# Empty bytes between the tiles in SBUF: weights and activations at multiples of 128 bytes

## The chip, the cores and the metric

The kernel runs on one core of one Trainium2 chip. The metric is the device time of one execution in microseconds, and the kernel before is given with the median of three runs. All arithmetic on the data happens on the chip; the host only puts the inputs into the order in which the chip reads them.

## The reference

What is computed is a trunk of two layers over 256 tokens of 2048 channels. Each layer has a modulation made from a vector `c`, a sub-layer with two attentions side by side, and a gated MLP with a short convolution over the tokens. Cut to what matters here:

```python
for l in range(2):
    mod = silu(c) @ ada_w[l] + ada_b[l]                    # 2048 x 12288
    sh_a, sc_a, gt_a, sh_m, sc_m, gt_m = split(mod, 6)
    h = rmsnorm(x, norm_mix[l]) * (1 + sc_a) + sh_a
    qa, ka, va, qb, kb, vb, ga, gb = split_cols(h @ w_in[l])   # 2048 x 8704
    ya = window_attention(...) @ w_proj_a[l]               # 8 heads, 2 key heads, rotary, sink
    yb = neighbourhood_attention(...) @ w_proj_b[l]        # 8 heads, learned bias
    x = x + gt_a * ((sigmoid(ga) * ya + sigmoid(gb) * yb) @ w_out[l])
    h = rmsnorm(x, norm_ffn[l]) * (1 + sc_m) + sh_m
    g, v = split(depthwise_conv(h @ w_up[l], conv_w[l], conv_b[l]))   # 2048 x 11264
    x = x + gt_m * ((silu(g) * v) @ w_down[l])             # 5632 x 2048
```

All inputs and the output are float32.

## The kernel before

**Products in two halves.** Every large product is made of 128 x 128 blocks of weights. A float32 number is split into a float32r half "hi" (a copy that the scalar engine rounds) and a rest "lo" (what the vector engine has left after subtracting hi). A block's product is then hi·hi + lo·hi + hi·lo, three products of 256 tokens. `unit` (line 216) loads 16 blocks, 1 MB, in one DMA to a tile `w` of pool `raw` (four buffers, 8192 bytes a partition each) and splits them into two tiles `hl` of pool `hl`, each 128 x 2 x 1024: line 225 is the copy on ScalarE, line 226 the subtraction on VectorE.

**Three forms of the product.**
- `feature_block` without `joint` (lines 239 to 243): the weights are the stationary operand, the activations the moving one. One matmul has 512 columns (hi of the weights with hi and lo of the activations, lines 240 and 242), the other 256 (lo of the weights with hi of the activations, lines 239 and 243). The two are called a pair below.
- `feature_block` with `joint` (lines 235 to 237): three matmuls of 256 columns into one place in PSUM. Most of layer 0's attention sub-layer is done so.
- `tokens` (lines 317 to 319): here 128 tokens of the activations are the stationary operand and 512 output features of the weights the moving one. q, k and v are made so.

The small products of the attention (`sc` line 465, `tp` line 490, `po` line 496, `qtp` line 453) are plain float32 without a split.

**Where operands lie.** Pools are laid out in SBUF one after the other in the order in which they are opened, and each tile takes its bytes rounded up to a multiple of 32. Ahead of the large tiles the pool `const` holds `ident`, `mean`, `mhalf` and the three tiles `cpad` of 1032 bytes, which end at byte 4896 of a partition. From there on nearly everything has a size that is a multiple of 128, so that all following tiles share one remainder; only pool `sm`, with its many tiles of 32 bytes, shifts the pool `s` behind it. The start addresses of the tiles, in bytes within a partition, with their remainders by 128:

| tile | pool | begins at | mod 128 |
|---|---|---|---|
| `ident` | const | 1152 | 0 |
| `cpad` 0, 1, 2 | const | 1728, 2784, 3840 | 64, 96, 0 |
| `cact`, `x` | const | 4896, 13088 | 32 |
| `w`, `aw` (four buffers) | raw | 37920 and on | 32 |
| `hl` (four buffers) | hl | 70688 and on | 32 |
| `h`, `merged` | h | 103456 | 32 |
| `u`, heads 6 and 7 of `oA`, `z`, `r` | ev | 136224 and on | 32 |
| `qsq`, `qn`, `p`, `pT`, `bias` | at | 147488 and on | 32 |
| `oA` (heads 0 to 5), `oB`, `act`, `ya`, q, k and v (`pack`) | s | 163296 and on | 96 |

Blocks within `hl` lie 512 bytes apart, hi and lo 4096; the channels' chunks of `h`, `merged`, `act`, `oA` and `oB` lie 2048 bytes apart, their hi and lo 1024. So each operand of a matmul has the remainder of its tile.

**Order of the work.** Layers, and stages within a layer, follow one another: q, k, v and gates A (in layer 0 in four parts of the rows, since its modulation is still on its way), projection A, gates B, projection B with the merge, `w_out`, and three groups of up and down of the MLP. The modulation (`ada`, line 152) is a product with a vector on VectorE (line 162, a 1 MB load `aw` each), 192 in all, spread over the units of weights by `ADA_PLAN_0` and `ADA_PLAN_1`. The steps of the attention are spread over units too (`Paced`). All loads are issued from SyncE's queue, in the order in which the program asks for them, and `w` and `aw` share the four buffers of `raw`.

Of the kernel before, what the change touches and what calls it, by code (L numbers as in the profile page):

```python
# [9 lines left out]
F32 = mybir.dt.float32  # L10
# [5 lines left out]
P = 128  # L16
# [15 lines left out]
# w_in's columns in groups of 512, in the order of use: k|v of A, q of A, then k, v, q of B by halves  # L32
QKV_GROUPS = [1024, 0, 512, 2560, 3584, 1536, 3072, 4096, 2048]
GATE_A, GATE_B = 4608, 6656
# the FFN's chunks of 128 channels, in groups that are kept on chip between up and down
FF_SIZES = [15, 16, 13]
FF_GROUPS = [list(range(sum(FF_SIZES[:i]), sum(FF_SIZES[: i + 1]))) for i in range(3)]
# the row blocks of q, k, v and mixer A's gates in the parts that are summed at a time: the first layer's modulation
# is still on its way
K_PARTS_0 = [2, 4, 5, 5]  # L40
K_PARTS = [[range(sum(K_PARTS_0[:i]), sum(K_PARTS_0[: i + 1])) for i in range(len(K_PARTS_0))], [range(KC)]]
# the output chunks of w_out and w_down that are worked on at a time: the first ones leave time for the last inputs
FIRST_TURN = 3
OUT_TURNS = [range(0, FIRST_TURN)] + [[mo] for mo in range(FIRST_TURN, KC)]
# chunks of the modulation that are done at a unit of weights, by layers, as corners of a line over the units
ADA_PLAN_0 = [(38, 32), (58, 48), (76, 66), (84, 70), (96, 80), (128, 96), (145, 108), (175, 118), (192, 124), (230, 143)]
ADA_PLAN_1 = [(0, 143), (76, 169), (84, 165), (95, 176), (129, 192)]
# layers whose mixer's products are summed in one place, for want of time on the vector engine
JOINT = [True, False]
# the same, with h, for the first layer's first chunks  # L50
# [3 lines left out]
# products without use that keep the tensor engine's clock up while it waits: before sums, their spread, and h  # L54
# [6 lines left out]
# heads of attention per unit of weights  # L61
ATT = [1.288, 0.4]
ATT_B = [0.21, 0.21]
# the order of the modulation's columns, in chunks of 128
# [4 lines left out]
def block_stream(l):  # L69
    """A layer's weights as (matrix, row block, column block of 128), in the order of use."""  # L70
    seq = []
    for part in K_PARTS[l]:
        for g in QKV_GROUPS:
            for kc in part:
                seq += [("w_in", kc, g // P + j) for j in range(4)]
        for mo in range(KC):
            seq += [("w_in", kc, GATE_A // P + mo) for kc in part]
    for mo in range(KC):
        seq += [("w_proj_a", kc, mo) for kc in range(HA)]
    for mo in range(KC):  # L80
        seq += [("w_in", kc, GATE_B // P + mo) for kc in range(KC)]
    for mo in range(KC):
        seq += [("w_proj_b", kc, mo) for kc in range(HB)]
    for mos in OUT_TURNS:
        seq += [("w_out", kc, mo) for kc in range(KC) for mo in mos]
    for gi, chunks in enumerate(FF_GROUPS):
        cols = [c + h * FC for c in chunks for h in range(2)]
        if gi == 0:
            for kc in range(KC):
                seq += [("w_up", kc, m) for m in cols[:4]]  # L90
            cols = cols[4:]
        for m in cols:
            seq += [("w_up", kc, m) for kc in range(KC)]
        for mos in OUT_TURNS:
            seq += [("w_down", kc, mo) for kc in chunks for mo in mos]
    return seq
# [8 lines left out]
def encoder(ctx: ExitStack, tc: tile.TileContext, a: dict, out: bass.AP):  # L105
    nc = tc.nc
    pool = lambda name, bufs, **kw: ctx.enter_context(tc.tile_pool(name=name, bufs=bufs, **kw))
    const = pool("const", 1)
# [17 lines left out]
    for i in range(3):  # L126
        t = const.tile([P, S + 2], F32, name=f"cpad{i}")
        nc.vector.memset(t[:], 0.0)
        cpad.append(t)

# [13 lines left out]
    x = const.tile([P, KC, S], F32, name="x")  # L144
    sp = pool("s", 1)
# [6 lines left out]
    def ada(l):  # L152
        """mod[l] = silu(c) @ ada_w[l] + ada_b[l], 128 columns a step, with the columns on partitions"""
        mod = lay.tile([P, 96], F32, name=f"mod{l}", tag="mod")
        ab = load(a["ab"][l], [P, 96], f"ab{l}", lay, tag="ab")
        nrm = load(a["nrm"][l], [P, 2, KC], f"nrm{l}", lay, tag="nrm")
        amod = lay.tile([P, 2, KC], F32, name=f"amod{l}", tag="amod")
        mods[l], amods[l] = mod, amod
        for n, i in enumerate(ADA_ORDER):
            raw = rawp.tile([P, D], F32, name=f"aw{l}_{n}", tag="raw")  # L160
            nc.sync.dma_start(raw[:], a["aw"][l, n])
            nc.vector.tensor_tensor_reduce(  # L162
                out=raw[:], in0=raw[:], in1=cact[:], scale=1.0, scalar=ab[:, i : i + 1],
                op0=ALU.mult, op1=ALU.add, accum_out=mod[:, i : i + 1],
            )
            part, kc = divmod(i, KC)
            if part in (1, 4):
                w = part // 3
                nc.vector.scalar_tensor_tensor(
                    out=amod[:, w, kc : kc + 1], in0=mod[:, i : i + 1], scalar=1.0, in1=nrm[:, w, kc : kc + 1],  # L170
                    op0=ALU.add, op1=ALU.mult,
                )
            done[l] = n + 1
            yield

    class Paced:
        """Steps of generators spread over the units of weights."""
# [4 lines left out]
        def defer(self, fn):  # L182
            """Puts a step off to the next unit"""
            self.later.append(fn)
# [31 lines left out]
    def unit(l, u):  # L216
        """A unit of weights: loaded, and split in two float32r halves (as they are wanted)."""
        raw = rawp.tile([P, UB * P], F32, name=f"w{l}_{u}", tag="raw")
        nc.sync.dma_start(raw[:], a["ws"][l, u])
        halves = []  # L220
        for j in range(2):
            n = UB * P // 2
            hl = hlp.tile([P, 2, n], F32R, name=f"hl{l}_{u}_{j}", tag="hl")
            r = raw[:, j * n : (j + 1) * n]
            nc.scalar.copy(hl[:, 0], r)  # L225
            nc.vector.tensor_tensor(out=hl[:, 1], in0=r, in1=hl[:, 0].bitcast(F32), op=ALU.subtract)  # L226
            halves.append(hl)
        return halves

    def feature_block(ps, hl, j, act, first, last, joint):  # L230
        """One 128 x 128 block: ps[:, :256] += hi.hi + lo.hi, and ps[:, 256:] (or the same place, if joint) += hi.lo."""
# [13 lines left out]
    class Stream:  # L245
        """The layer's units, in order; act(kc) is [P, 2, S] (hi, lo)."""
# [8 lines left out]
        def feed(self, i):  # L255
            """Has the steps of the coming inputs made, a few ahead"""
            while self.steps and self.fed <= i + FEED:
                if next(self.steps, bg) is bg:
                    self.steps = None
                self.fed += 1  # L260

        def prefetch(self, n):
            """Units that are split before what follows"""
            for _ in range(n):
                self.ahead.append(unit(self.l, self.u + len(self.ahead)))

        def hold(self, ins, n):
            """The next n units' splits follow an instruction"""
            self.after = (ins, self.u + len(self.ahead) + n)
# [21 lines left out]
        def features(self, acts, evacs, late=None, joint=False):  # L291
            """Some blocks of 128 output features over the given K blocks, side by side; late() near their end."""
# [13 lines left out]
        def tokens(self, h, kcs):  # L306
            """512 output features of all tokens over the given K blocks, tokens on partitions."""
# [25 lines left out]
    def warm(n):  # L333
        """Products without use: the tensor engine's clock falls when it waits for long"""
        if n:
            ps = ax.tile([P, 512], F32, name="warm", tag="ax")
            for _ in range(n):
                tc.keep_in_program_order(nc.tensor.matmul(ps[:, :P], ident[:], ident[:], start=True, stop=True))

    class Squares:  # L340
        """The tokens' mean squares of x, chunk by chunk; the last one's are apart"""
# [25 lines left out]
    def rsqrt(dst, src, n, k):  # L367
        """dst = (src / n + eps) ** -0.5, in place of a table's square root"""
# [3 lines left out]
    def normed(l, w, sums, st, first=False):  # L372
        """rmsnorm(x) * norm * (1 + scale) + shift, split in halves: the tile, and the steps that fill it"""
# [39 lines left out]
    def qk_rows(pss, heads, rot, gain, dst, then):  # L413
        """q or k of some heads: rmsnorm, rotary, to dst [P (channels), heads, S], a step per unit"""
# [46 lines left out]
    def attend(qT, kT, v, mask, scale, sink, o):  # L461
        """One head, in three steps: o [P (channels), 2, S] from qT, kT [P (channels), S] and v(key block) [P (tokens), channels]"""
# [53 lines left out]
    def plan(l, u):  # L516
        """Goes on with the modulation as planned for a layer's unit"""
# [6 lines left out]
    def need(l, n):  # L524
        """Goes on with the modulation up to the n-th chunk of a layer"""
        while done[l] < n:
            next(adas)

    def ada_and_h(steps):
        """The first layer's modulation, and h chunk by chunk behind it"""  # L530
# [12 lines left out]
    # the tokens' mean squares of the first x  # L543
# [16 lines left out]
    def small(l):  # L560
        """A layer's small inputs"""
# [20 lines left out]
    for l in range(L):  # L582
# [15 lines left out]
        # q, k, v: k|v and q of A, then k, v, q of B by halves  # L598
# [38 lines left out]
        def attention():  # L637
            """The heads' steps, those of a few heads at a time, the oldest head first"""
# [22 lines left out]
        for pi, part in enumerate(parts):  # L661
# [38 lines left out]
            # mixer A's gates  # L700
# [14 lines left out]
        # merge of the branches  # L715
        joint = JOINT[l]

        def whole(ps):
            """The sum of a bank's halves"""
# [42 lines left out]
        def residual(ps, mo, part, joint):  # L762
            """x += gate * ps"""
# [26 lines left out]
        # channel mixer  # L790
# [154 lines left out]
```

## Time and profile before

| | |
|---|---|
| median of 3 runs | 2792.53 us (2791.72 to 2793.07) |
| span of the profiled execution | 2791.1 us |
| instructions | 39852 |
| VectorE busy | 2216.8 us (79%) |
| ScalarE busy | 1449.7 us (52%) |
| DMA | 699.72 MB, 251 GB/s over the span |

The span runs from the first to the last instruction of one profiled execution; the median is of other executions without a profile. A profile of this kernel is best read by stages, since the loads of the modulation and the three forms of the product make each stage different. Rows of matmuls give a start and a modelled duration; successive matmuls overlap, so that the time which one takes is read from the distance between starts.

### The profile page before, as it was taken

The page shows a single profiled execution, that of the slowest core. Times are in us where ns is not written, and L with a number is a line of the kernel's source. Part 1 is how long each engine was busy: PE and PEld are TensorE (multiplying, and loading weights), DVE is VectorE, ACT ScalarE, POOL GpSimd, SP SyncE. Part 2 cuts the span into 40 slices and gives each one's busy share as a digit, 9 for nine tenths or more (in the row PEclk, how much of TensorE's full clock was granted, in tenths as well). Part 3 has the DMA queues.
Part 4 walks back from the last instruction along what each step waited for, and adds up shares of the span by engine and source line. Part 5 has one row for each costly group of instructions (what it writes and reads, how often), then busy time and mean ns, then how long its engine had stood idle before and what let it go on. Part 6 is the DMA issues. An engine that isn't in the chain of part 4 may idle for free.

```text
span 2791.1 us, 39852 instructions
## 1 busy us (share of the span) xinstructions
PE 2734.8 (98%) x15930; PEld 2398.0 (86%) x15930; DVE 2216.8 (79%) x3163; ACT 1449.7 (52%) x2137; POOL 39.3 (1%) x24
## 2 busy tenths in 40 slices
PE   7899999999999999999999999999999999999999
PEld 5788899998888888888878888888878888888888
DVE  6998987897998888789876666768889757766775
ACT  5334784444654555355444567545455535543553
POOL 0000100000000000000000000000000000000000
PEclk9999999999999999999999999999999999999999
DMA  8886588896778766677756666575768655555553
GB/s 313 336 331 254 221 304 326 328 341 231 287 277 320 267 251 252 253 282 282 279 198 238 226 224 238 215 269 195 294 231 290 230 194 181 187 190 181 189 189 136
DMA packets 101852, 699.72 MB, mean 251 GB/s; under 512 B 12705, under 2 KB 15009, under 8 KB 17697
## 3 DMA queue, kind: packets, MB, share of 16 engines
q1 hardware_dynamic: 101666, 697.17, 67.8%
q8 instruction: 125, 2.05, 0.3%
q14 instruction: 61, 0.50, 0.0%
HBM read 695.03 MB, written 2.10 MB: 250 GB/s over the span
## 4 chain that ended last, share of the span: by engine, by line
PE 79%; issue 14%; DVE 4%; POOL 1%; DMA 1%; ACT 1%; POOLq 0%; SPq 0%; DVEq 0%
PE ps L242 33%; PE ps L243 17%; PE ps_t L318 4%; PE ps_t L319 4%; PE ps_t L317 4%; PE ps L236 4%; PE ps L235 4%; PE ps L237 4%; PE ps L240 2%; DVE aw L162 1%; PE ps L239 1%; DVE hl L226 1%; POOL qrs L370 1%; PE sc L465 1%; PE po L496 0%
## 5 line engine op out<-in xcount | busy, mean ns | idle before, releaser
L226 DVE TENSOR_TENSOR hl<-w,hl 128x1024 fp32r<-128x1024 f32 x928 | 1131.8, 1223 | 319.7 <-ACT hl L225 314.5
L225 ACT CAST hl<-w 128x1024 fp32r<-128x1024 f32 x928 | 973.3, 1051 | 778.2 <-PE ps L243 249.0
L242 PE MATMUL ps<-h,hl 128*128 128x512 f32 x3120 | 1113.1, 400 | 0.9 <-DVE h L406 0.9
L243 PE MATMUL ps<-h,hl 128*128 128x256 f32 x3120 | 877.8, 281 | 0.0
L242 PEld LDWEIGHTS ps<-h,hl 128*128 128x128 f32 x3120 | 588.0, 188 | 136.7 <-DVE h L406 1.5
L243 PEld LDWEIGHTS ps<-h,hl 128*128 128x128 f32 x3120 | 590.7, 189 | 9.3
L162 DVE CUSTOM_DVE_ANT_0 aw<-aw,cact,ab 128x2048 f32<-128x2048 f32 x192 | 450.7, 2347 | 19.5 <-DMA aw<-in_aw 19.3
L326 ACT COPY r<-ps 128x256 f32<-128x256 f32 x240 | 89.1, 372 | 302.1 <-PE ps L240 301.9
L317 PE MATMUL ps_t<-hl,h 128*128 128x512 f32 x576 | 228.3, 401 | 7.5 <-ACT hl L225 7.0
L318 PE MATMUL ps_t<-hl,h 128*128 128x512 f32 x576 | 228.8, 397 | 4.7 <-DVE hl L226 4.7
L319 PE MATMUL ps_t<-hl,h 128*128 128x512 f32 x576 | 227.4, 395 | 0.9 <-DVE h L406 0.9
L242 PE MATMUL ps<-act_o,hl 128*128 128x512 f32 x496 | 177.5, 397 | 0.0
L806 DVE SCALAR_TENSOR_TENSOR u<-cpad,cw,u 128x256 f32<-128x256 f32 x352 | 169.1, 482 | 4.8 <-ACT u L804 0.4
L766 DVE SCALAR_TENSOR_TENSOR x<-ps,mod,x 128x256 f32<-128x256 f32 x237 | 111.6, 481 | 47.8 <-PE ps L240 37.4
L237 PE MATMUL ps<-h,hl 128*128 128x256 f32 x512 | 146.1, 285 | 0.0
L235 PE MATMUL ps<-h,hl 128*128 128x256 f32 x512 | 145.4, 284 | 0.0
L236 PE MATMUL ps<-h,hl 128*128 128x256 f32 x512 | 145.2, 284 | 0.0
L243 PE MATMUL ps<-act_o,hl 128*128 128x256 f32 x496 | 139.7, 282 | 0.0
L242 PE MATMUL ps<-act_b,hl 128*128 128x512 f32 x384 | 136.8, 397 | 0.0
L317 PEld LDWEIGHTS ps_t<-hl,h 128*128 128x128 f32 x576 | 109.7, 191 | 31.1 <-ACT hl L225 7.6
L318 PEld LDWEIGHTS ps_t<-hl,h 128*128 128x128 f32 x576 | 110.1, 191 | 30.6 <-DVE hl L226 8.1
L319 PEld LDWEIGHTS ps_t<-hl,h 128*128 128x128 f32 x576 | 109.9, 191 | 24.2 <-DVE h L406 1.4
(214 smaller groups left out, 3998.0 us busy)
## 6 DMA issues: line engine op xcount, KB each, us to landing
w<-in_ws SPq DMA_DIRECT2D x464, 1024.0 KB, 4.9
aw<-in_aw SPq DMA_DIRECT2D x192, 1024.0 KB, 4.9
bias<-in_bias SPq DMA_DIRECT2D x16, 256.0 KB, 4.5
x<-in_xT SPq DMA_DIRECT2D x4, 512.0 KB, 5.6
out<-x SPq DMA_DIRECT2D x16, 128.0 KB, 1.8
cw<-in_cw SPq DMA_DIRECT2D x2, 176.0 KB, 4.5
maskA<-in_maskA SPq DMA_DIRECT2D x1, 256.0 KB, 7.5
ab<-in_ab SPq DMA_DIRECT2D x2, 48.0 KB, 6.1
```

What stands on the lines that cost most here:

```text
L162: nc.vector.tensor_tensor_reduce(out=raw[:], in0=raw[:], in1=cact[:], scale=1.0, scalar=ab[:, i : i + 1], op0=ALU.mult, op1=ALU.add, accum ...
L225: nc.scalar.copy(hl[:, 0], r)
L226: nc.vector.tensor_tensor(out=hl[:, 1], in0=r, in1=hl[:, 0].bitcast(F32), op=ALU.subtract)
L235: nc.tensor.matmul(out[:, 0], hi, act[:, 0], start=first, stop=False)
L236: nc.tensor.matmul(out[:, 0], hi, act[:, 1], start=False, stop=False)
L237: nc.tensor.matmul(out[:, 0], lo, act[:, 0], start=False, stop=last)
L242: nc.tensor.matmul(out, hi, act, start=first, stop=False)
L243: nc.tensor.matmul(out[:, 0], lo, act[:, 0], start=False, stop=False)
L317: nc.tensor.matmul(ps[:], xh, hi, start=kc == kcs[0], stop=False)
L318: nc.tensor.matmul(ps[:], xh, lo, start=False, stop=False)
L319: nc.tensor.matmul(ps[:], xl, hi, start=False, stop=kc == kcs[-1])
L806: nc.vector.scalar_tensor_tensor(out=u, in0=pad[:, o : o + S], scalar=w[:, j : j + 1], in1=u, op0=ALU.mult, op1=ALU.add)
```

## The change

Two tiles that hold nothing of use are put in: one of 96 bytes at the end of the small constants, behind `cpad`, and one of 64 bytes in a pool of its own, opened after all pools but `s`. Each is filled with zeros once by VectorE. Everything behind the first moves by 96 bytes, pool `s` by 160 bytes. Comments and docstrings are taken out of the file as well, with blank lines in their place; lines behind the new ones move by 7 to 9.

```diff
+    skips = []
+
+    def skip(n, p=None):
+
+        skips.append((p or pool(f"skip{len(skips)}", 1)).tile([P, n // 4], F32, name=f"skip{len(skips)}"))
+        nc.vector.memset(skips[-1][:], 0.0)
+
     const = pool("const", 1)
...
         nc.vector.memset(t[:], 0.0)
         cpad.append(t)
+    skip(96, const)
...
     x = const.tile([P, KC, S], F32, name="x")
+    skip(64)
     sp = pool("s", 1)
```

With the second pool opened behind `sm`, the addresses become: `cact` 4992, `w` 38016 and on, `hl` 70784 and on, `h` 103552, `s` 163456 and on. All of them are multiples of 128, and none of them is one of 256.

## The prediction

> **What bounds the kernel now.** I read the page's busy times and its chain of waits first, then the busy times in stretches, then the order of time inside single stretches, for the distance between the starts of matmuls.
>
> ```profile
> PE 2734.8 (98%) x15930; PEld 2398.0 (86%) x15930; DVE 2216.8 (79%) x3163; ACT 1449.7 (52%) x2137; POOL 39.3 (1%) x24
> ...
> PE 79%; issue 14%; DVE 4%; POOL 1%; DMA 1%; ACT 1%; POOLq 0%; SPq 0%; DVEq 0%
> ```
>
> TensorE is busy nearly always, and the chain that ended last is TensorE's, with some other engine for 7% of it. Busy in stretches (columns: length; busy time and count of TensorE, weight loads, VectorE, ScalarE, GpSimd; granted clock; DMA share; GB/s):
>
> ```profile
> 28.00:420.00 392.00, 372.45 (x2146) 325.31 (x2147) 352.32 (x559) 221.22 (x357) 15.87 (x7) 0.98 0.78 290
> 420.00:660.00 240.00, 240.00 (x2025) 239.88 (x2024) 201.63 (x246) 105.09 (x133) 0.00 (x0) 1.00 0.87 325
> 660.00:710.00 50.00, 44.39 (x251) 38.47 (x250) 44.01 (x77) 29.36 (x50) 2.74 (x1) 0.93 0.55 204
> 710.00:960.00 250.00, 250.00 (x1419) 217.17 (x1418) 222.56 (x296) 126.56 (x176) 0.00 (x0) 1.00 0.79 292
> 960.00:1260.00 300.00, 300.00 (x1702) 260.56 (x1701) 248.09 (x340) 154.13 (x218) 0.00 (x0) 1.00 0.71 260
> 1260.00:1380.00 120.00, 120.00 (x681) 104.17 (x680) 107.57 (x149) 65.07 (x97) 0.00 (x0) 1.00 0.76 279
> 1380.00:1500.00 120.00, 113.49 (x564) 96.19 (x563) 89.81 (x136) 55.19 (x77) 6.22 (x3) 0.96 0.59 218
> 1500.00:1660.00 160.00, 160.00 (x752) 133.56 (x751) 108.35 (x170) 90.32 (x148) 8.18 (x5) 1.00 0.61 226
> 1660.00:2030.00 370.00, 370.00 (x2120) 323.24 (x2118) 276.56 (x401) 209.52 (x330) 0.00 (x0) 1.00 0.66 245
> 2030.00:2300.00 270.00, 264.39 (x1491) 229.13 (x1489) 215.60 (x309) 139.63 (x201) 2.74 (x1) 0.99 0.64 232
> 2300.00:2791.00 491.00, 487.19 (x2775) 423.61 (x2773) 334.04 (x465) 243.13 (x343) 0.00 (x0) 1.00 0.50 180
> ```
>
> In most stretches TensorE has no idle time at all at a granted clock of 1.00, so only a faster matmul shortens them. Only 28 to 420 us shows much idle time, with VectorE at 90%. What a matmul costs stands in the timeline (start, duration, engine, line): token products, pairs, joint products from `h`, joint products from `oB`, and the end of those from `oA`.
>
> ```profile
> 1500.14 0.39 PE L317 MATMUL ps_t<-hl,h 128*128 128x512 f32 x1
> ...
> 1503.54 0.39 PE L317 MATMUL ps_t<-hl,h 128*128 128x512 f32 x1
> ```
>
> ```profile
> 1000.27 0.40 PE L242 MATMUL ps<-h,hl 128*128 128x512 f32 x1
> ...
> 1003.80 0.40 PE L242 MATMUL ps<-h,hl 128*128 128x512 f32 x1
> ```
>
> ```profile
> 479.82 0.28 PE L237 MATMUL ps<-h,hl 128*128 128x256 f32 x1
> ...
> 480.90 0.28 PE L237 MATMUL ps<-h,hl 128*128 128x256 f32 x1
> ```
>
> ```profile
> 539.73 0.28 PE L236 MATMUL ps<-oB,hl 128*128 128x256 f32 x1
> ...
> 542.00 0.28 PE L235 MATMUL ps<-oB,hl 128*128 128x256 f32 x1
> ```
>
> ```profile
> 430.38 0.28 PE L235 MATMUL ps<-oA,hl 128*128 128x256 f32 x1
> ...
> 431.10 0.28 PE L235 MATMUL ps<-oA,hl 128*128 128x256 f32 x1
> ...
> 432.80 0.28 PE L235 MATMUL ps<-oA,hl 128*128 128x256 f32 x1
> ```
>
> Between the two rows shown lie 15 token products (3.40 us, **226.7 ns** each), 10 pairs (3.53 us, **353.0 ns**), 9 joint products from `h` (1.08 us, **120.0 ns**) and 20 from `oB` (2.27 us, **113.5 ns**). In `oA`, 6 products take 0.72 us (120 ns) and the next 15 take 1.70 us (113.3 ns): of the eight chunks just two, heads 6 and 7, lie in pool `ev` at remainder 32, the others in pool `s` at 96, and six of 24 products are slow (the slow ones lag those two chunks by some three products).
>
> So one line, one size, one clock and the same weights run at two speeds, and what differs is where in SBUF the moving operand begins. From 512 and 256 columns a column takes (226.7 - 120.0) / 256 = 0.4168 ns, so 512 columns stream in 213.4 ns and 256 in 106.7. The rest is a surplus: 13.3 ns of a token product, 13.3 of a joint product from `h`, 6.8 from `oB`, and 353.0 - 320.1 = 32.9 of a pair. They come near to 2, 2, 1 and 5 times 6.7 ns, and 6.7 ns is the time of 16 columns, 64 bytes of float32r. An operand that begins 32 bytes past a multiple of 64 touches one more piece of 64 bytes than an aligned one. Plain float32 products, at misplaced addresses too, show what is left without such a surplus (rows of the chain, four matmuls each, of 256 and of 128 columns):
>
> ```profile
> 1557.38 0.86 PE po L496 x4
> 1558.25 0.44 PE tp L490 x4
> ```
>
> That is 215 and 110 ns, a column in 0.82 ns, close to twice 0.4168; over 213.4 and 106.7 ns stand 1.6 and 3.3 ns, some 2.5. At half the column rate the same remainder of 32 costs next to nothing, at the full rate 6.7 ns and multiples: what I would expect of reading that is short only at the full rate.
>
> **The change part by part.** (1) *Matmuls.* No row shows a float32r product whose operands both begin at a multiple of 64. The bounds: nothing lost or won (the surplus has other causes), and the whole surplus gone. I take a surplus of 2.5 ns as in the float32 rows, since the two speeds of one line are the nearest evidence that the place sets the surplus: token 215.9, joint 109.2, pair 325.1 ns. A product wins 10.8 ns in tokens and joint, 27.9 / 2 = 13.9 in pairs. By the stretches, with the small float32 products taken out of the counts:
> - 28 to 420: some 1906 products x 10.8 = 20.6 at most. VectorE is at 352.3 of 392 and waits with latency stand between; I take 8.
> - 420 to 660: 240 - 2025 x 0.1092 = 18.9 at most, less what DMA forbids (below): 12.
> - 660 to 710: 212 x 13.9 = 3. 960 to 1260: 1702 x 13.9 = 23.7, VectorE then at 90%.
> - 710 to 960: 1419 x 13.9 = 19.7, and VectorE would stand at 97%. If it holds at 95%, 222.6 / 0.95 = 234.3, so 15.7. 1260 to 1380 likewise: 9.5, with 107.6 / 0.95 only 6.8.
> - 1380 to 1500: some 190 in pairs and 290 in tokens, 5.8, less for its waits: 5. 1500 to 1660: 570 in tokens, 52 in pairs: 7.
> - 1660 to 2030: 28. 2030 to 2300: 20.5. 2300 to 2791: 38.6. VectorE stays below 87% in all three.
>
> The DMA of 420 to 660 has its own row (TensorE alone, clock, DMA share, GB/s):
>
> ```profile
> 440.00:520.00 80.00, 80.00 (x669) 1.00 0.94 345
> ```
>
> At a share of 0.94 these 80 us can win about 1 us, not 7; hence 12 for the stage.
>
> Sum: 8 + 12 + 3 + 15.7 + 23.7 + 6.8 + 5 + 7 + 28 + 20.5 + 38.6 = **168.3 us**. The span of 2791.1 becomes 2622.8; the median lies 1.4 us above the span, so **2624 us**. Without the caps it is 195; without any surplus, 2.5 x 12,100 products = 30 more, 2792.5 - 225 = 2567. With VectorE held to 90%, the most that a stretch above shows, 28 to 420 wins nothing, 710 to 960 2.7 and 1260 to 1380 0.5, 27 less in all: 2651.
>
> (2) *VectorE, ScalarE, DMA.* Two additions show whether VectorE minds the place: line 327 writes to `cpad` one element past its start (remainders 68, 100, 4), line 827 works on `u` at 32.
>
> ```profile
> L327 DVE TENSOR_TENSOR cpad<-ps,r 128x256 f32<-128x256 f32 x176 | 74.4, 425 | 68.6 <-ACT r L326 68.5
> ...
> L827 DVE TENSOR_TENSOR u<-u 128x256 f32<-128x256 f32 x88 | 37.3, 424 | 2.1
> ```
>
> 425 and 424 ns: I take nothing for VectorE, and nothing for ScalarE, whose 52% is never the bound. A transfer of 8192 bytes a partition gains or loses at most one piece of 64 bytes in 128, 0.8%; that touches only the 80 us above, under 1 us either way.
>
> (3) *The two fills*, of 24 and 16 columns:
>
> ```profile
> 0.84 0.07 DVE L124 MEMSET mhalf<- 128x8 f32 x1
> 0.92 0.82 DVE L128 MEMSET cpad<- 128x258 f32 x3
> ...
> 1.71 0.17 DVE L139 MEMSET one<- 1x128 f32 x1
> ...
> 2.54 5.45 PE L142 MATMUL cb<-cact,one 1*128 1x512 f32 x6 [2.54 <-DMA cact<-in_c]
> ```
>
> Between 0.07 and 0.27 us each, I take 0.1. The first stands ahead of `one` on VectorE, which ends at 1.88 while the first matmul waits for a DMA until 2.54: covered by 0.66 us, and 0.1 to 0.2 us without that cover.
>
> [...]
>
> **The rivals.** *Half of it goes*: each product keeps one 6.7 ns, as `oB`'s do (something of a float32r weight load or restart). A pair then takes 333.5, token products 220.1, joint 113.4. The stages give 4 + 8 + 39 + 4 + 4 + 19 + 14 + 27 = 119: 2673 us. For it: no float32r row shows less than 113.3.
>
> *Nothing changes*: the surplus of pairs is 32.9 with operands of `s` as with those of `h`, so it may belong to the alternation of 512 and 256 columns; and 128 may be no better than 32 if the unit were 256 bytes. Against it: the two speeds of one line, and the 64 bytes in the sizes. 2792.7 with the fills.
>
> *Slower*: what costs may be that moving operand and weights begin at the same remainder. `h` and `hl` share 32 and take 120; `oB` at 96 with `hl` at 32 takes 113.5. After the change all share one. If every product from pool `s` pays 6.7 more: 1408 blocks of `w_down` and 224 of layer 1's projections as pairs, two products each, and 672 joint ones: 3936 x 6.7 = 26 us, 2819. It decides the sign above 840 such products; with the joint ones alone, 4.5 us, it is lost in the noise. Against it: token products share a remainder and pay no more than joint ones from `h`; pairs from `s` do not share one and pay as much.
>
> **How the numbers follow.** The full gain 0.57; half of it 0.20; a smaller part (6.7 off each product, 72 to 77 us, some 2718) 0.07; nothing 0.09; slower 0.07. The range from 2560 to 2735 holds the first three, with the bounds 2567 and 2651 of the first. About 0.2% can be told from no change here: faster 0.84, same 0.09, slower 0.07.
>
> **What would show it.** Joint products, from `h` and `oB` alike, at about 109 ns, token products at 216, pairs at 325, in stretches without idle time; VectorE's durations unchanged at 425 ns; layer 1's stretches shorter by 8%, and 710 to 960 and 440 to 520 by less, with waits for VectorE and DMA there. A pair still at 353 makes the forecast wrong, 333 gives the first rival; joint products from `oB` at 120 give the last.

## The result and the profile after

| | median us (runs) | ratio to the kernel before, 95% interval |
|---|---|---|
| before | 2792.22 (20) | |
| with the empty bytes | 2795.27 (20) | 1.0014 [1.0008, 1.0020] |

The kernel is about 0.1% slower: 3.05 us by the medians, outside the noise. The prediction (2624 us, faster) is wrong. The profiled execution has a span of 2793.3 us. The same stretches as in the prediction, after (length; busy time and count of TensorE, weight loads, VectorE, ScalarE, GpSimd; clock; DMA share; GB/s):

```profile
420.00:660.00 240.00, 240.00 (x2002) 240.00 (x2001) 201.12 (x245) 102.28 (x132) 0.00 (x0) 1.00 0.86 321
710.00:960.00 250.00, 250.00 (x1421) 217.42 (x1420) 223.28 (x299) 127.33 (x179) 0.00 (x0) 1.00 0.80 294
2030.00:2300.00 270.00, 265.30 (x1492) 230.60 (x1491) 216.52 (x309) 139.00 (x201) 2.74 (x1) 0.98 0.64 234
```

In the two stretches of pairs TensorE does what it did (1421 products against 1419, 1492 against 1491). In 420 to 660 it does 23 products fewer in the same time. Which ones shows in shorter stretches that hold one form and one moving operand each. First the kernel before, then the kernel after, TensorE alone (busy time and count, clock, DMA share, GB/s):

```profile
440.00:520.00 80.00, 80.00 (x669) 1.00 0.94 345
530.00:565.00 35.00, 35.00 (x311) 1.00 0.83 302
...
720.00:840.00 120.00, 120.00 (x681) 1.00 0.79 287
...
2320.00:2480.00 160.00, 160.00 (x908) 1.00 0.51 184
```

```profile
440.00:520.00 80.00, 80.00 (x669) 1.00 0.93 349
530.00:565.00 35.00, 35.00 (x294) 1.00 0.83 294
...
720.00:840.00 120.00, 120.00 (x681) 1.00 0.80 289
...
2320.00:2480.00 160.00, 160.00 (x908) 1.00 0.53 187
```

Since TensorE is busy without a break here, length over count is the time of a product. Joint products from `h` (440 to 520) stay at 119.6 ns. Joint products from `oB` (530 to 565) go from 112.5 to 119.0 ns. Pairs from `h`, in the last two stretches, stay at 176.2 ns a product, 352.4 a pair. A stretch of pairs from pool `s`, before and then after:

```profile
2485.00:2555.00 70.00, 70.00 (x399) 1.00 0.52 186
```

```profile
2485.00:2555.00 70.00, 70.00 (x398) 1.00 0.50 182
```

With two more such stretches (2225 to 2285 and 2720 to 2765) 999 products take 175 us, before as after: these pairs stay too, at 350.4 ns. Of all that the change moved, one thing shows: `oB`'s products, and those of `oA` from pool `s`, 672 together, became as slow as those from `h`. At 6.5 ns each that is 4.4 us, against 3.05 by the medians (2.2 to 5.6 by the interval).

### The profile page after: what moved, and what is told of

Same layout as the page of the kernel before. It is cut to its first block, busy times and chain, and to the rows that moved or that the text cites. A ratio compares the mean times of both kernels' runs of the same rounds, so it can differ in the third digit from the quotient of the medians.

```text
span 2793.3 us, 39854 instructions
## 1 busy us (share of the span) xinstructions
PE 2737.5 (98%) x15930; PEld 2401.1 (86%) x15930; DVE 2217.0 (79%) x3165; ACT 1448.5 (52%) x2137; POOL 39.3 (1%) x24
## 4 chain that ended last, share of the span: by engine, by line
PE 79%; issue 14%; DVE 4%; POOL 1%; ACT 1%; DMA 1%; POOLq 0%; SPq 0%; DVEq 0%; ACTq 0%
PE ps L251 33%; PE ps L252 17%; PE ps_t L327 4%; PE ps_t L328 4%; PE ps L246 4%; PE ps L245 4%; PE ps L244 4%; PE ps_t L326 4%; PE ps L249 2%; DVE aw L171 1%; PE ps L248 1%; DVE hl L235 1%; POOL qrs L379 1%; PE sc L474 1%; PE po L505 1%
## 5 line engine op out<-in xcount | busy, mean ns | idle before, releaser
L235 DVE TENSOR_TENSOR hl<-w,hl 128x1024 fp32r<-128x1024 f32 x928 | 1132.0, 1223 | 318.8 <-ACT hl L234 312.7
L234 ACT CAST hl<-w 128x1024 fp32r<-128x1024 f32 x928 | 973.3, 1050 | 793.4 <-PE ps L252 250.8
L326 PEld LDWEIGHTS ps_t<-hl,h 128*128 128x128 f32 x576 | 109.4, 190 | 31.5 <-ACT hl L234 8.3
L327 PEld LDWEIGHTS ps_t<-hl,h 128*128 128x128 f32 x576 | 109.2, 190 | 30.3 <-DVE hl L235 8.1
L336 DVE TENSOR_TENSOR cpad<-ps,r 128x256 f32<-128x256 f32 x176 | 74.5, 425 | 70.7 <-ACT r L335 70.3
```

The source lines that it names most:

```text
L326: nc.tensor.matmul(ps[:], xh, hi, start=kc == kcs[0], stop=False)
L327: nc.tensor.matmul(ps[:], xh, lo, start=False, stop=False)
```

## The experiments

What the one changed row suggests: before, pool `s` began 64 bytes (modulo 128) from where the weights begin, and `h` 0 bytes; after, all lie at distance 0. Distance is the start of the activations less the start of the weights. So the two speeds may belong to the distance between the two operands of a product (**theory R**), not to the place of each (**theory A**, on which the prediction rested).

**One part of the change at a time.** The first kernel has only the 96 bytes, the second only the 64 (both diffs against the kernel after).

```diff
     x = const.tile([P, KC, S], F32, name="x")
-    skip(64)
     sp = pool("s", 1)
```

> Only the 96 empty bytes, so weights, h and all else begin at multiples of 128, but pool s (oA, oB, act) at 64 past one: 64 from the weights, as in the kernel before. Theory R (the distance between moving operand and weights, modulo 128, sets the surplus of joint products): joint products from oB back at 113.3 ns, time as before, 2792. Theory A (the place of each operand by itself counts, and 0 is no better than 32): oB begins at a multiple of 64, like h, so 120 ns, time as with the whole change, 2795.

```diff
         nc.vector.memset(t[:], 0.0)
         cpad.append(t)
-    skip(96, const)
```

> Only the 64 empty bytes ahead of pool s: weights, h and pool s all begin 32 past a multiple of 128. Theory R: joint products from oB at 120 ns, and the time of the whole change, 2795, though nothing is aligned. Theory A (the place of s at 96 was the good one, or the alignment costs): with s at 32 the joint products from oB take 120 too, but the other part of the loss, if the move to multiples of 128 has any, is missing.

Measured: only the first part 2791.59 us (ratio 1.0000 [0.9992, 1.0009]), only the second 2796.33 us (1.0012 [1.0003, 1.0021]). Their rows for the joint products from `oB`, first part alone, then second part alone:

```profile
530.00:565.00 35.00, 35.00 (x311) 1.00 0.81 300
```

```profile
530.00:565.00 35.00, 35.00 (x294) 1.00 0.80 290
```

The kernel that has weights and `h` at multiples of 128 behaves as before, to the product. The kernel in which nothing is aligned behaves as with the whole change. The alignment does nothing; the 64 bytes ahead of pool `s` carry the whole loss, by bringing `s` to distance 0 from the weights. Theory R holds in both. Theory A fails in the first, where it wants 120 ns for `oB`; the second does not decide, since theory A too wants 120 there.

**The other way round: h brought away from the weights** (against the kernel before, with its function `skip` added).

```diff
     hlp = pool("hl", 4)
+    skip(64)
     hp = pool("h", 1)
...
+    skip(64)
     sp = pool("s", 1)
```

> 64 empty bytes between the weights' tiles and h, and 64 ahead of pool s: the weights begin 32 past a multiple of 128, h, merged, the tiles of ev and pool s all at 96: every moving operand is 64 bytes from the weights. Theory R: joint products from h and merged go from 120 to 113.3 ns, some 2350 of them x 6.7 = 16 us off, 2776; token products, if they follow the same rule, from 226.7 to 220 with some 6 more off outside the stretches that VectorE bounds; pairs stay at 353. Theory A: 120 ns stays for h (96 is as far from a multiple of 64 as 32), time 2792 to 2795.

Measured: 2789.49 us, ratio 0.9985 [0.9974, 0.9996]. Stretches of joint products from `h`, from `oB`, and of pairs:

```profile
440.00:520.00 80.00, 80.00 (x682) 1.00 0.93 351
530.00:565.00 35.00, 35.00 (x300) 1.00 0.80 300
...
2320.00:2480.00 160.00, 160.00 (x913) 1.00 0.52 188
```

Joint products from `h` take 117.3 ns, better than 119.6 but not the 113.3 that was expected; those from `oB`, also at 64 now, 116.7 instead of 112.5. In the kernel before `s` lies 448 from the weights modulo 512, here 64. Either 64 and 448 differ, or a distance does not always give one speed; what comes below speaks for the second. Joint products gained a third of what was expected, and token products take 233 ns at 64 bytes against 227 at 0 in the groups alone, below, so the 16 us were not reached. Pairs gained 1 ns a product.

**Products alone.** The next kernel runs groups of products back to back, each with its operands at chosen bytes.

```diff
+    for n, (name, form, wo, ho) in enumerate(GROUPS):
+        wo, ho = wo // 4, ho // 4
+        hl = W[:, wo : wo + 2048].rearrange("p (a n) -> p a n", a=2)
+        hf = H[:, ho : ho + 8192]
+        h = hf.rearrange("p (k a s) -> p k a s", k=KC, a=2)
...
+            if form == "joint":
+                mat(o2[:, 0], hi, act[:, 0], start=first, stop=False)
+                mat(o2[:, 0], hi, act[:, 1], start=False, stop=False)
+                mat(o2[:, 0], lo, act[:, 0], start=False, stop=last)
```

> Leaves out the whole computation; TensorE works through groups of float32r products alone, in the forms of the kernel, with the weights and the moving operand at chosen bytes of two tiles that begin at multiples of 256 with a distance that is a multiple of 512. Groups of joint products (48 each) at distances 0, 32, 64 and so on to 512 with the weights at 0; at distances 0 and 64 with the weights at 32 and 64; and with 4 and 16. The same for pairs (32 products in a group), for pairs with the operands written as one run of 512 columns, for two products of 512 columns, for token products, for joint products that all use one block of weights. Theory R: joint 120 ns at distance 0 and at multiples of 128, 113.3 at 64 and perhaps at others, whatever the start of the weights. Theory C (the other engines' reads and writes of SBUF make the surplus): with TensorE alone all groups stand near 109 ns, tokens near 216 and pairs near 325. Theory F (a fixed cost of a float32r product or weight load): 120, 227 and 353 in all groups.

Joint groups with weights and moving operand at 0 and 448; 0 and 512; 32 and 32; 32 and 96; 64 and 64; 64 and 0 (the letters o to t; start, length, 48 products; the next group's start ends a group):

```profile
94.67 5.63 PE L181 MATMUL joint_o<-H,W 128*128 128x256 f32 x48
100.14 5.90 PE L181 MATMUL joint_p<-H,W 128*128 128x256 f32 x48
105.88 5.91 PE L181 MATMUL joint_q<-H,W 128*128 128x256 f32 x48
111.63 5.82 PE L181 MATMUL joint_r<-H,W 128*128 128x256 f32 x48
117.29 5.92 PE L181 MATMUL joint_s<-H,W 128*128 128x256 f32 x48
123.04 5.62 PE L181 MATMUL joint_t<-H,W 128*128 128x256 f32 x48
128.50 6.08 PE L181 MATMUL joint_u<-H,W 128*128 128x256 f32 x48
```

Start to start over 48: distance 448 and -64 (the same modulo 512) take 114.0 and 113.8 ns, distance 0 takes 119.6, 119.8 and 119.8 whether both begin at 0 (or 512), 32 or 64, distance 64 takes 117.9. No other engine works here, but for ScalarE's copy of one column after each group, so theory C (reads and writes by others make the surplus) falls: the kernel's own figures come out with TensorE alone. An aligned float32r product, the row that the prediction lacked, takes 120 ns and not 109. Theory F has the level right, and theory R the differences. Pairs with the operands written as one run of columns took what pairs in the kernel's form take (352.5 to 353.1 ns against 351.9 to 352.5 at the same starts), and joint products on one block of weights what others take (119.6 ns at distance 0; at 448, in the next kernel, they took 126.0). Starts that are not multiples of 32 stand apart: 123.1 ns at distance 4, 116.9 at 16, and 118.3 with both operands at 16. A stream of products of 128 columns takes 110.0 ns each at distance 0 (3.52 us for 32), 56.7 over the 53.3 of its columns, so that something other than its columns holds up so short a product.

**448 for h.** As two places above, with more bytes between the weights and `h`.

```diff
-    skip(64)
+    skip(448)
     hp = pool("h", 1)
```

> 448 empty bytes between the weights' tiles and h, and 64 ahead of pool s: h, merged, the tiles of ev and pool s all begin 448 bytes past the weights, modulo 512, as pool s does in the kernel before (joint 113.5 ns) and as the groups alone at 448 and at -64 do (114.0 and 113.7). Nothing is aligned: weights at 32 past a multiple of 128, the rest at 96. Theory R512 (the distance modulo 512 between the two operands of a product sets the surplus): joint products from h and merged at 113.5 to 114 instead of 120 ns, 2350 x 6.3 = 15 us off; token products, whose operands are swapped, unknown between 227 and 234 (the groups alone at other distances), that is 0 to 12 us lost; pairs near 353. Time 2777 to 2790. Theory A (alignment): 2792 to 2795, h at 120.

Measured: 2791.12 us, ratio 0.9995 [0.9985, 1.0004]: no change by the runs, and just outside the expected range. Its joint products from `h`:

```profile
440.00:520.00 80.00, 80.00 (x708) 1.00 0.95 361
```

113.0 ns, as expected; token products take 229 ns at 448 bytes in the groups alone, below. That profiled run took 2783.4 us, but the median of the runs shows no gain: the eleven runs spread from 2782.2 to 2794.4, those of the kernel before beside it only from 2789.0 to 2793.3. The groups alone, below, suggest why: some distances have two speeds.

**All distances, and what the surplus belongs to.**

```diff
+            elif form == "three":
+                mat(ps[:, :384], hi, flat[:, :384], start=first, stop=False)
+                mat(ps[:, :384], lo, flat[:, :384], start=False, stop=last)
+            elif form == "half":
+                mat(ps[:], Wb[:, j * P : (j + 1) * P], Hb[:, kc % 8 * 512 : (kc % 8 + 1) * 512], start=first, stop=False)
...
```

> Leaves out the whole computation; groups of products alone as before, now joint, pair and token at each distance from 0 to 480 bytes in steps of 32, joint at 432, 464 and 496, and for what the surplus belongs to: products of 384 columns, of 512 columns at distance 448, bfloat16 products of 512 columns, plain float32 products of 512 columns, and products of 128 columns at 448. Theory R512: joint lowest near 448 and within 113 to 124 elsewhere, with 64 and 192 unlike 448 although all are odd multiples of 64. Theory W (each weight load takes some of the moving operand's reads, a fixed time for a product): 384 columns at 160 + 13 = 173 ns, 512 at 227, and products of 128 columns at the weight load's own 110. Theory B (float32r moves 4 bytes a column at the full rate and that is what is short): bfloat16 near 216 ns for 512 columns, plain float32 near 429 with no surplus.

By the starts of the groups, ns of a product (for pairs, of both), weights at 0:

| distance, bytes | 0 | 32 | 64 | 96 | 128 | 160 | 192 | 224 | 256 | 448 |
|---|---|---|---|---|---|---|---|---|---|---|
| joint | 120 | 118 | 118 | 120 | 119 | 119 | 118 | 118 | 120 | 118 |
| pair | 347 | 347 | 352 | 350 | 351 | 347 | 353 | 352 | 353 | 352 |
| token | 227 | 233 | 233 | 234 | 232 | 234 | 229 | 233 | 227 | 229 |

The other distances repeat those 256 lower to within 1.3 ns, but for pairs at 0 and 256; so in this kernel the period is 256 bytes, not 512. In the first of these kernels it was not so for joint products: 192 took 117.9 ns and 448 took 114.0. Two distances show two speeds: joint at 448 took 114.0 ns there and 118 here, and a pair at distance 0 took 353 there (5.64 us for 16) and 347 here. No distance tried, alone or in a kernel, takes a joint product below 112. What the surplus belongs to (384 columns at distance 0 and 448, 512 columns at 448, bfloat16, 512 columns, then plain float32):

```profile
401.24 5.71 PE L195 MATMUL three_a<-H,W 128*128 128x384 f32 x32
406.79 5.70 PE L195 MATMUL three_b<-H,W 128*128 128x384 f32 x32
412.33 7.63 PE L195 MATMUL wide_a<-H,W 128*128 128x512 f32 x32
419.80 7.08 PE L195 MATMUL half_a<-Hb,Wb 128*128 128x512 bf16 x32
426.71 13.90 PE L195 MATMUL plain_a<-x 128*128 128x512 f32 x32
```

A float32r product of 384 columns takes 5.55 / 32 = 173.4 ns, 13.4 over the 160 of its columns, like 256 (120) and 512 (227) at distance 0: from 256 columns on, the surplus at this distance is a fixed time for a product, not a share of its columns. At 448 it is 13.1 for 384 and 20 for 512 (7.47 / 32 = 233.4). A bfloat16 product of 512 columns takes 6.91 / 32 = 215.9 ns, 2.5 over 213.4. Plain float32 takes 13.34 / 32 = 417 ns by the starts of its group and the next, not over twice 213.4; the program asks for 16 such products and the trace has 32 records, so that is half of a product. Float32r has the surplus; bfloat16 with its 2.5 ns has little of it, plain float32 none. Theory B names these two, but a rate that is short would cost more with more columns, and at distance 0 it does not.

**Shorter weight loads.** Does the weight load beside a product take the time? Then fewer columns of weights should cost less.

```diff
+            elif form == "wq":
+                mat(ps[:32, :512], hi[:, :32], flat[:, :512], start=first, stop=False)
+                mat(ps[:32, :512], lo[:, :32], flat[:, :512], start=False, stop=last)
...
```

> Leaves out the whole computation; groups of 32 products alone with 512 or 256 moving columns and weights of 128, 96, 64 or 32 columns, at distances 0, 32 and 128. Theory W (the weight load beside a product takes the surplus from the moving operand's reads): the surplus falls with the weights: over 213.4 ns some 13.3 at 128 columns, 10 at 96, 6.7 at 64, 3.3 at 32, and the same over 106.7 for 256 columns where the load is short enough. Theory F (a fixed cost of each float32r product): 13.3 ns whatever the weights.

Weights of 128, 96, 64 and 32 columns with 512 moving columns, at distance 0:

```profile
25.84 7.45 PE L157 MATMUL wf_a<-H,W 128*128 128x512 f32 x32
33.13 7.53 PE L157 MATMUL wt_a<-H,W 128*96 128x512 f32 x32
40.49 7.52 PE L157 MATMUL wh_a<-H,W 128*64 128x512 f32 x32
47.84 7.58 PE L157 MATMUL wq_a<-H,W 128*32 128x512 f32 x32
55.26 3.99 PE L157 MATMUL jf_a<-H,W 128*128 128x256 f32 x32
59.08 3.87 PE L157 MATMUL jt_a<-H,W 128*96 128x256 f32 x32
```

228, 230, 230 and 232 ns: with 512 moving columns the surplus does not shrink with the weights, nor in any order at the other distances (227 to 233 ns). Theory W falls in this form. With 256 moving columns a product went from 119.4 ns (3.82 / 32, between the last two rows) to 113.4 with 32 columns of weights at distance 0, half of its surplus, and stayed at 117 to 120 at distances 32 and 128. Some 7 to 20 ns remain with every float32r product in these groups, whatever the weights' length.

**Distances chosen by stage.** `h` becomes a part of a tile with 192 bytes to spare, so that each stage can begin it where its form of product does best. The first kernel moves layer 0's first `h` and `merged`, the second the three tensors of the pairs, the third all five. Pool `s` is at 192 in all three.

```diff
+    AWAY = {'h0_0': 192, 'merged0': 192, 'h0_1': 32, 'h1_0': 0, 'merged1': 32, 'h1_1': 32}
+
+    def h_tile(name):
+        n, o = KC * 2 * S, AWAY[name] // 4
+        t = hp.tile([P, n + 48], F32R, name=name, tag="h")
+        return t[:, o : o + n].rearrange("p (k a s) -> p k a s", k=KC, a=2)
...
+    skip(64)
     sp = pool("s", 1)
```

> h is a part of a tile with 192 bytes to spare, so that it can begin at 0, 32 or 192 past the weights, modulo 256, by layer and stage. Here only layer 0's first h and merged, the moving operands of nearly all joint products, lie 192 away; the other h and merged at 0, pool s and ev at 192. Theory R256 with W (each product loses 13.3 ns to the weight load beside it, and the distance modulo 256 moves that by up to 6.7 ns either way): joint products from h and merged at 113.5 to 118 instead of 120 ns, 5 to 15 us off; layer 0's token products at 229 to 232 instead of 227, mostly hidden beside VectorE, 0 to 3 us lost; pairs as before. 2779 to 2789. Theory A (alignment): 2792.

> The same tiles; layer 0's h of the MLP and layer 1's merged and h of the MLP, the moving operands of some 3040 pairs, lie 32 away from the weights, all others of pool h at 0. Theory R256 with W, by the groups alone (pairs 350.8 ns at 32, in the kernel before 353 at 0): 2.5 ns off each, 7 us, 2785; the surplus of pairs stays, since no group came under 350 ns. Theory A: 2792.

> Both: layer 0's first h and merged 192 away, the three tensors of pairs 32 away. Theory R256 with W: the two gains add, 12 to 22 us off, 2770 to 2780, faster than both kernels and with nothing aligned to 64 bytes.

| | median us (runs) | ratio, 95% interval |
|---|---|---|
| joint at 192 | 2787.45 (10) | 0.9979 [0.9969, 0.9990] |
| pairs at 32 | 2778.11 (5) | 0.9948 [0.9936, 0.9961] |
| both | 2772.56 (5) | 0.9930 [0.9918, 0.9941] |

The third, in the stretches of joint products from `h` and of the MLP's pairs in both layers:

```profile
440.00:520.00 80.00, 80.00 (x682) 1.00 0.93 353
...
720.00:840.00 120.00, 120.00 (x692) 1.00 0.81 293
...
2320.00:2480.00 160.00, 160.00 (x920) 1.00 0.53 190
```

Pairs go from 352.4 to 347.8 ns; some 3040 of them make 14 us, and the second kernel is 13.7 us faster than the 2791.79 beside it. That is twice the 7 us expected, which went by 350.8 ns for pairs at 32; the starts of the groups give 347.5 and 346.9. The joint products took 117.3 ns in this profile, where 113 was seen with 448 for `h`; the runs of the first kernel spread from 2778.8 to 2791.6. With both, the kernel is 19 us faster than before, beats both kernels, and its tiles are no better aligned than before.

The first two kernels also show two speeds at one place. Pool `s` and the weights have the same addresses in both, and only `h` and `merged` differ; yet their joint products from `oB` took 116.7 ns in the first and 112.2 in the second:

```profile
530.00:565.00 35.00, 35.00 (x300) 1.00 0.84 298
```

```profile
530.00:565.00 35.00, 35.00 (x312) 1.00 0.81 301
```

So the distance alone does not settle a speed between 112 and 118 ns. What does is not shown. At distance 0, with starts at multiples of 32, every profile has 119 to 120, but for the first group in each kernel of groups (149 to 167 ns). The ten runs of the first kernel fall into 2779 to 2782 us (four) and 2786 to 2792 (six), and 2350 joint products at 4 ns make 9 us; so an execution may have one speed or the other throughout, but no second profile shows it.

## Why the prediction was wrong

- **What bounds the kernel** was read rightly: TensorE without idle time in most stretches. All that the experiments gained came from shorter products there.
- **The step that failed** is the one from "one line at two speeds" to "an operand that begins 32 bytes past a multiple of 64 touches one more piece of 64 bytes" (no run shows such a piece), and with it the surplus of 2.5 ns taken for aligned operands. Aligned joint products take 119.6 to 120 ns, aligned token products 227, pairs 352: a surplus of 13 to 16 ns a product and not 2.5, so that nothing of the 168.3 us came. The two speeds did depend on the place, but on the distance between the two operands: groups at 0 and 0, 32 and 32, 64 and 64 take the same time, and distances 64 and 448 take less. The rows allowed both readings, since `oB` differed from `h` in its own remainder and in its distance from `hl` at once.
- **Sizes that fit by chance.** The surplus came in multiples of 6.7 ns, and that is 64 bytes of float32r. But it is a fixed 13 ns for a product of 256, 384 or 512 columns at distance 0, and moves by up to 7 ns with the distance. That a misplaced plain float32 product has none was taken for a sign of misplacement at full rate; an aligned float32r product has it all the same. The 2.5 ns came from rows that could not show it: a record of `po` is half of a product (64 products, 128 records), and the 110 ns of `tp` are also what a float32r product of 128 columns takes, whose columns alone would need 53.3. The 109.2 ns forecast for a joint product of 256 columns is less than even that.
- **The rival that came true is the slower one**: moving operand and weights at the same distance. Its place (joint products from `oA` and `oB`) and their 113.5 to 120 ns are measured, and its price for them alone, 4.5 us, stands against 3.05. The larger form, 26 us with the pairs from pool `s`, did not happen: those pairs stayed at 350.4 ns. The prediction judged the small form lost in the noise; 20 runs tell it apart. What it held against this rival was right as far as it went: the pairs from `s` did not follow the rule, and token products are even fastest at distance 0 (227 ns, up to 234 elsewhere).
- **The first rival**, half of it goes, fell with the forecast. *Nothing changes* was right for all other products. Its first reason, the alternation of 512 and 256 columns, explains little: streams of one width alone have 13 ns a product at distance 0, 27 for two, and a pair has 33 at 353 ns and 27 at 347.
- **VectorE, ScalarE** were read rightly. The subtraction of `unit` takes 1223 ns before and after, the addition in `u` 424, ScalarE's copy in `unit` 1051 before and 1050 after. VectorE's rows after, in the groups of instructions (busy us, mean ns):

```profile
L235 DVE TENSOR_TENSOR hl<-w,hl 128x1024 fp32r<-128x1024 f32 x928 | 1132.0, 1223 | 318.8 <-ACT hl L234 312.7
...
L836 DVE TENSOR_TENSOR u<-u 128x256 f32<-128x256 f32 x88 | 37.4, 424 | 2.1
```

- **The fills** cost what was said and are covered (timeline after):

```profile
1.70 0.08 DVE L113 MEMSET skip<- 128x24 f32 x1
1.74 0.17 DVE L147 MEMSET one<- 1x128 f32 x1
1.86 0.07 DVE L113 MEMSET skip<- 128x16 f32 x1
...
2.48 1.19 PE L150 MATMUL cb<-cact,one 1*128 1x512 f32 x1 [2.48 <-DMA cact<-in_c]
```

- **The caps** were not put to the test by this change. The one on DMA was too tight: with 448 bytes the stretch of 440 to 520 did 708 products at 361 GB/s and a share of 0.95, 6% more than the 669 that were taken to be near the limit.

## What to carry to other kernels

Before a speed is put down to where an operand begins, list the starts of both operands of the product: here the distance between them was worth up to 7 ns of a float32r product, and the alignment of either, in multiples of 32 bytes, nothing. A surplus has no floor that can be claimed until some row or a run of products alone shows one without it. Groups of products alone, in kernels of under half a millisecond, gave a map that paid 0.7% in the kernel; as speeds at one distance can differ between kernels, what the map promises is to be measured there.

## What the runs showed of the hardware

At distance 0 a float32r matmul takes 13 ns more than its columns, whether they are 256, 384 or 512 (one of 128 takes 57 ns more); a bfloat16 one of 512 takes 2.5 ns more. With fewer columns of weights the surplus of 512 moving columns does not shrink (14 ns with 128, 18 with 32), and that of 256 halves at distance 0 (12.7 ns with 128, 6.7 with 32). The distance between moving operand and weights changes it: joint products between 112 and 120 ns, token products between 227 and 234, pairs between 347 and 353, at multiples of 32 bytes. At some distances the same products ran at two speeds in two kernels (groups of joint products at 448: 114.0 and 118 ns; pairs at 0: 353 and 347; `oB` at 192: 116.7 and 112.2). The kernels with `h` away from 0 for joint products spread by 11 to 14 us from run to run, the kernel before by 4 to 7.5; that the one makes the other is argued, not shown. Why float32r pays this, why the distance matters, and what picks one of two speeds stays open: these runs show it with TensorE alone and rule out, for 512 columns, the length of the weight load, no more.
